# One layer step of a hybrid decoder on one core: x loaded on SyncE's queue, a shorter root in two norms, another order of x1's blocks, unread products, dt's sums in three steps

## The chip, the core and the metric

The kernel runs on one core of a Trainium2 chip. The core has a matmul engine (TensorE, PE in the profile, with its weight loads shown apart as PEld), and VectorE (DVE), ScalarE (ACT) and GpSimd (POOL) for the work on elements; SyncE (SP) only issues transfers. Each engine takes its own instructions in order, and semaphores order the engines against each other. DMA queues belong to the engine that issues into them (SP's, ACT's and POOL's are used here). SBUF and PSUM are the memories on the core: a matmul writes PSUM, which has eight banks in this kernel, four in a pool for the large products (`mm`) and four for the rest (`ms`).

The metric is the device time of one execution in microseconds (us), shorter is better.

## The reference

One step of one layer for 256 prompt tokens and 8 × 8 sample tokens, 320 in all, with a width of 2048, float32 throughout:

```python
h = rms_norm(x, norm_mix_pre)
u, v, z, xbc, dt = split(h @ w_in)            # 2048, 2048, 2048, 3072, 32 columns
gate, chunk_v = chunk_spatial_gate(u, v, ...)  # gelu, layer norm of v, products inside chunks of 128
ssm, states = ssd_mixer(z, xbc, dt, ...)       # conv of 4, softplus of dt, chunked scan, gated norm
x = x + rms_norm(concat(gate, ssm) @ w_out, norm_mix_post)
f = conv_ffn(rms_norm(x, norm_ffn_pre))        # up to 2 x 5632, conv of 3, gelu(g) * u, down to 2048
x = x + rms_norm(f, norm_ffn_post)

def rms_norm(x, w): return x * rsqrt(mean(x * x) + 1e-6) * w
```

Outputs are x, the states of the scan, the last rows of the convolutions and of v.

## The kernel before

Activations lie transposed: 128 of the 2048 features on the partitions, 16 such blocks (kt 0 to 15), the 320 tokens along a row. A product with float32 weights is made from two halves of each operand in the reduced type fp32r: x = hi + lo, w = hi + lo, and `accumulate` (L126) issues three matmuls per block, w_hi·x_hi (L128), w_hi·x_lo (L129) and w_lo·x_hi (L130), each 128 × 128 by 128 × 320. Weights come in slabs by `slab` (L110): SP loads `wraw` (512 KB, or 256 KB for the first four), ACT casts it to `whi` (L117), DVE subtracts to get `wlo` (L119). Each of the three has three buffers, so SP's issue of a slab waits until the slab three before it is split, and the cast waits until PE has used the slab three before.

`project` (L152) multiplies all 16 blocks of the split activations (`h_hi`, `h_lo`) into 4 banks, 2 blocks and 24 matmuls per slab; with `more` it fills 6 banks, and a third slab for every two then serves the two others. `ready` is called ahead of each slab and makes the blocks of activations that the slab needs. `chunk_out` (L199) multiplies 4 blocks of a mixer or FFN result into the 16 blocks of `acc`. Work of the other engines and small products run as background generators, which `tick` moves one step (one `yield`) after a slab. A list scheduler orders each engine's instructions by priority (`first()` and `high_priority` raise it), and `issue_after` adds an order that the data doesn't ask for.

The places that matter here, in order of time:

- **The start.** PE runs `EARLY` matmuls on ones. ACT's queue gets x in six pieces (L526: 1, 1, 2, 4, 4 and 4 blocks, the tile `vt`), SP's the slabs. `x_ready` (L533) scales and splits a block into `h_hi` (ACT, L537) and `h_lo` (DVE, L538) for V0, the first projection (192 matmuls). The norm's factor r1 isn't in these: it's applied when the banks are read out, so V0 can start at once. r1 comes from x by tokens, which POOL loads by `load_by_token` (L548), four pieces of 512 KB and two of 256 KB (`bT`, `cT`), behind `h_hi` of block 8; `with_r1` squares and sums them and spreads r1.
- **dt.** `steps` (L414) makes the step sizes and then three groups of small products: prefix sums `cs_ps` (L463), the same transposed `csT_ps` (L478), and the sums after each token `dec_ps` (L491). A `yield` stands between some of these.
- **Norm 2.** The last `chunk_out` of the mixer calls `squares_of` per block: ACT squares, POOL adds; the last three blocks go a faster way, and block 15's square (L297) stands alone in `one`. `token_sums` (L258) sums both tiles over the features with three small matmuls each (`tsum`), `rsqrt_by_root` (L237) makes 1/sqrt by ACT's Sqrt and one correcting step on DVE, `spread` (L267) turns it into a row by three transposes. `root_table` (L252) activates a Sqrt on one element. A product of the scan's final state (`fin_ps`, L877) and its sum (L879) lie between.
- **x1.** `x1_ready` (L975) makes block kt of x1 = x + norm 2: DVE multiplies (L980), then adds the block of x (`xr`, loaded by SP; DVE for blocks 0 and 1, POOL for the others, L981), then `split` (ACT L346, DVE L347). The first `project` of the FFN takes these as they come, 288 matmuls in 6 banks, with one slab of `ahead`, so blocks 0 and 1 and then 2 and 3 are made together.
- **Norm 3.** The squares of x1 go half to `sq3` (added on POOL) and half to `sq3b` (DVE). `ffn_up(0)` (L1002) multiplies one further bank (`ps_one`, 48 matmuls), takes the sums and the root, reads the banks out with the factor r3, and multiplies the last one (`ps_other`).
- **`renewals`** (L1085), the renewal of the sample states, runs in the background of the FFN. Its tile `kept` has the tag of the mixer's `ohi`, and so its memory; ACT scales parts of it (L1118), and the raw loads come from `xq_d`.
- **The tail.** Norm 4 goes like norm 2, with products `x1p` that bring x1 into PSUM; DVE and POOL finish the blocks and SP and ACT store them.

## Time and profile before

| | |
|---|---|
| runs of the kernel | 1811.83 us median of 3 (1809.76 to 1812.11) |
| the profiled execution | 1812.42 us |
| its span in the trace | 1810.7 us |
| mean granted clock of TensorE | 0.993 |
| matmuls (L128 to L130 alone) | 0.31 us each, pipelined |
| DMA | 306.46 MB, 169 GB/s on the mean |

The span is what the profiler saw from the first to the last instruction; the profiled execution took 1.7 us more than that. Two things in the views need care. Matmuls overlap, so the duration of one (0.31 us) is about twice the distance from one to the next. And "granted clock" is the share of TensorE's full clock that the chip's throttle allowed: 0.50 means that every matmul took about twice as long, with no idle time shown. In a row of the stretches, the columns are the stretch, its length, the busy time and the instructions of PE, PEld, DVE, ACT and POOL, the granted clock, the DMA engines' busy share and GB/s. In a timeline row they are start, duration, engine, line, operation, tiles and shapes, count, and the idle time before it with what ended it. In a row of the costliest groups, the mean duration in ns stands behind the busy time.

### The profile page before, as it was taken

The numbers are of one execution on the slowest core, as the hardware profiler recorded it, in microseconds if no ns is written. First come the engines' busy times: TensorE is split into PE (matmuls) and PEld (weight loads), VectorE is DVE, ScalarE is ACT, GpSimd is POOL, SyncE is SP. The second block draws the span as 40 slices with busy tenths as digits, with TensorE's granted clock in tenths as the row PEclk, the third lists the DMA queues.
The fourth block names the chain that finished last, engine by engine and source line by source line (L and its number), as shares of the span: only waits on it lengthen the run. The fifth ranks groups of instructions, "written<-read, shape, count | busy, mean of one in ns | idle before, by whom it ended". The sixth has DMA issues, their size and how long they took to land.

```text
span 1810.7 us, 31220 instructions
## 1 busy us (share of the span) xinstructions
PE 1784.3 (99%) x12222; PEld 1750.2 (97%) x12222; DVE 1183.4 (65%) x2033; ACT 798.7 (44%) x1106; POOL 303.2 (17%) x624
## 2 busy tenths in 40 slices
PE   8999999999999999999999999999999999999998
PEld 7999999999999898998899999999999999999997
DVE  4449565556867778577776575757665565756575
ACT  6444454334535354445455444344434343433335
POOL 2102110000120111005622212121201020101004
PEclk9999999999999999999999999999999999999999
DMA  8545544445764644454556656565654444444442
GB/s 269 178 149 176 173 137 152 152 151 162 244 197 154 192 161 150 137 178 150 161 163 201 196 191 211 174 202 177 194 175 151 147 153 150 155 152 153 149 153 99
DMA packets 229779, 306.46 MB, mean 169 GB/s; under 512 B 17440, under 2 KB 152704, under 8 KB 229440
## 3 DMA queue, kind: packets, MB, share of 16 engines
q1 hardware_dynamic: 216384, 279.26, 48.5%
q10 hardware_dynamic: 11024, 18.10, 2.7%
q0 software_dynamic: 2224, 7.11, 1.4%
q8 instruction: 96, 1.57, 0.4%
q14 instruction: 51, 0.42, 0.1%
HBM read 286.85 MB, written 17.58 MB: 168 GB/s over the span
## 4 chain that ended last, share of the span: by engine, by line
PE 93%; DVE 2%; DMA 2%; ACT 1%; POOL 1%; issue 1%; ACTq 0%; DVEq 0%; POOLq 0%
PE ps L128 19%; PE ps L130 19%; PE ps L129 19%; PE pd L128 10%; PE pd L130 10%; PE pd L129 10%; DMA wraw<-in_w_in 1%; PE y_ps L851 1%; DVE wlo L119 1%; POOL acc_mix L981 1%; PE yo_ps L804 1%; ACT whi L117 0%; PE sg L658 0%; PE up_ps L1128 0%; PE xt_ps L357 0%
## 5 line engine op out<-in xcount | busy, mean ns | idle before, releaser
L119 DVE TENSOR_TENSOR wlo<-wraw,whi 128x1024 fp32r<-128x1024 f32 (+1 forms) x476 | 591.4, 1243 | 409.1 <-ACT whi L117 406.1
L117 ACT CAST whi<-wraw 128x1024 fp32r<-128x1024 f32 (+1 forms) x476 | 496.8, 1044 | 721.1 <-PE ps L129 443.4
L128 PE MATMUL ps<-h_hi,whi 128*128 128x320 f32 x2528 | 790.2, 313 | 11.0 <-ACT whi L117 7.6
L130 PE MATMUL ps<-h_hi,wlo 128*128 128x320 f32 x2528 | 786.5, 311 | 4.0 <-DVE wlo L119 4.0
L129 PE MATMUL ps<-h_lo,whi 128*128 128x320 f32 x2528 | 785.1, 311 | 0.0
L128 PEld LDWEIGHTS ps<-h_hi,whi 128*128 128x128 f32 x2528 | 477.8, 189 | 17.6 <-ACT whi L117 9.2
L130 PEld LDWEIGHTS ps<-h_hi,wlo 128*128 128x128 f32 x2528 | 477.8, 189 | 6.1 <-DVE wlo L119 5.9
L129 PEld LDWEIGHTS ps<-h_lo,whi 128*128 128x128 f32 x2528 | 477.8, 189 | 1.2 <-issue 0.5
L128 PE MATMUL pd<-fhi,whi 128*128 128x320 f32 x704 | 218.0, 310 | 0.0
L129 PE MATMUL pd<-flo,whi 128*128 128x320 f32 x704 | 217.9, 310 | 0.0
L130 PE MATMUL pd<-fhi,wlo 128*128 128x320 f32 x704 | 217.9, 309 | 0.0
L128 PE MATMUL pd<-ohi,whi 128*128 128x320 f32 x448 | 140.6, 314 | 0.0
L129 PE MATMUL pd<-olo,whi 128*128 128x320 f32 x448 | 139.0, 310 | 0.0
L130 PE MATMUL pd<-ohi,wlo 128*128 128x320 f32 x448 | 138.7, 310 | 0.0
L129 PEld LDWEIGHTS pd<-flo,whi 128*128 128x128 f32 x704 | 132.2, 188 | 0.7
L130 PEld LDWEIGHTS pd<-fhi,wlo 128*128 128x128 f32 x704 | 132.2, 188 | 0.0
L128 PEld LDWEIGHTS pd<-fhi,whi 128*128 128x128 f32 x704 | 132.2, 188 | 0.0
L211 DVE TENSOR_TENSOR acc_ffn<-acc_ffn,pd 128x320 f32<-128x320 f32 x160 | 77.1, 483 | 35.8 <-PE pd L130 34.8
L1032 POOL COPY ptf<-pad 128x2 f32<-128x2 f32 x88 | 23.0, 263 | 390.7 <-DVE pad L1020 390.0
L128 PEld LDWEIGHTS pd<-ohi,whi 128*128 128x128 f32 x448 | 84.1, 188 | 4.0 <-issue 2.5
L130 PEld LDWEIGHTS pd<-ohi,wlo 128*128 128x128 f32 x448 | 84.1, 188 | 0.6 <-issue 0.6
L129 PEld LDWEIGHTS pd<-olo,whi 128*128 128x128 f32 x448 | 84.2, 188 | 0.2 <-issue 0.2
(296 smaller groups left out, 1596.1 us busy)
## 6 DMA issues: line engine op xcount, KB each, us to landing
wraw<-in_ffn_w_up SPq DMA_DIRECT2D x176, 512.0 KB, 3.5
wraw<-in_w_in SPq DMA_DIRECT2D x144, 512.0 KB, 3.5
wraw<-in_ffn_w_down SPq DMA_DIRECT2D x88, 512.0 KB, 3.3
wraw<-in_w_out SPq DMA_DIRECT2D x64, 512.0 KB, 3.3
st<-in_state_ssm SPq DMA_DIRECT2D x64, 256.0 KB, 3.7
out_ssm_state_sample<-st ACTq DMA_DIRECT2D x32, 256.0 KB, 2.5
cs<-dacs_d SPq DMA_DIRECT2D x16, 320.0 KB, 3.5
xr<-in_xT SPq DMA_DIRECT2D x4, 640.0 KB, 4.6
```

The lines of the kernel that those rows point to most:

```text
L117: act.copy(hi[:, :m], raw[:, :m])
L119: dve.tensor_tensor(out=lo[:, :m], in0=raw[:, :m], in1=hi[:, :m].bitcast(F32), op=ALU.subtract)
L128: pe.matmul(ps, whi, xhi, start=first, stop=False)
L129: pe.matmul(ps, whi, xlo, start=False, stop=False)
L130: return pe.matmul(ps, wlo, xhi, start=False, stop=last).ins
L211: dve.tensor_tensor(out=acc[:, nb, :], in0=acc[:, nb, :], in1=ps[:, :NT], op=ALU.add)
L804: pe.matmul(ps_yo[row:row + 32, :256], cms[:, 4 * h + i, :], st[h][:, 256 * r:256 * r + 256], start=i == 0, stop=i == 3, tile_position=(0, ...
L851: pe.matmul(ps[64 * i:64 * i + 64, cols], w(hl), x(hl, m, cpx), tile_position=(0, 64 * i), **flags)
L981: added.append((dve if kt < 2 else pool).tensor_tensor(out=a, in0=a, in1=xr[q][:, k, :], op=ALU.add).ins)
L1032: pool.tensor_copy(ptf[:, k, :], pad[:, 256:258])
```

## The change

It has seven parts.

1. `EARLY` is 8, and a tile `eps` holds the constant for Sqrt.
2. x is loaded inside `x_ready`, on SP's queue, each piece just ahead of the slab that needs it. The loads by token go to SP's queue too: one behind the x of block 8's slab, one behind that of 10, two behind that of 12, the last two after V0's. ACT and POOL issue none. `with_r1` gets a further `yield`.
3. `rsqrt_by_root` takes one sum, which `token_sums` accumulates in two calls (`more`). Sqrt reads it from PSUM with scale and bias, beside a multiply-add and a reciprocal on DVE, and three DVE operations follow. `root_table` is called behind the square of block 12, for both norms, and block 15's square is on DVE.
4. `unread(n)` issues n matmuls on an old mixer tile (`res[2]`), whose result nobody reads: 2 between the sums of norm 2, 11 behind its spread.
5. x1: block 0 is added before block 1 is multiplied (`issue_after(added[0])`), and all adds are on DVE.
6. The squares of x1 are one sum, added on DVE, behind the splits of blocks 11 and 15. In `ffn_up(0)` one bank is copied out by ACT, and spread and read-out stand inside the loop of `ps_other`.
7. dt: three more `yield`s, two ahead of the first sums and one behind them.

As scheduled, SP's order in the start is x0, w0, x1, w1, x2, w2, x3, w3, x4-5, w, x6-7, w, x8-9, w, token 0, x10-11, w, token 1, x12-15, w, tokens 2 and 3, w, `bT`. The prefix sums of dt stay at their place among PE's matmuls, the transposed sums come some 18 matmuls later, the others later still. `kept`'s two first loads stand on SP behind the FFN's fifth slab and ahead of x's third piece (blocks 8 to 11), and wait for PE; ACT has its scaling of `kept` between the splits of x1's blocks 1 and 2.

The diff, with the context cut:

```diff
@@ -26,7 +26,7 @@
...
 EPS = 1e-6
-EARLY = 10
+EARLY = 8
@@ -62,8 +62,10 @@
...
     ones = cp.tile([P, P], F32, name="ones")
+    eps = cp.tile([P, 1], F32, name="eps")
...
         dve.memset(ones, 1.0)
+        dve.memset(eps, EPS)
@@ -232,54 +234,50 @@
...
-    rsqrt_ins, sums_ins = [], []
-    def rsqrt_by_root(rest, ps, scale, rows=P):
-        v = tp.tile([P, 3], F32, tag="rs_v3", name="rs_v")[:rows]
-        r = tp.tile([P, 3], F32, tag="rs_r3", name="rs_r", bufs=3)[:rows]
-        t = tp.tile([P, 3], F32, tag="rs_t3", name="rs_t")[:rows]
-        s = tp.tile([P, 3], F32, tag="rs_s3", name="rs_s")[:rows]
-        dve.tensor_scalar(out=v, in0=rest, scalar1=scale, scalar2=EPS, op0=ALU.mult, op1=ALU.add)
-        dve.scalar_tensor_tensor(out=v, in0=ps, scalar=scale, in1=v, op0=ALU.mult, op1=ALU.add)
-        act.activation(s, v, AF.Sqrt)
-        dve.reciprocal(r, s)
-        dve.scalar_tensor_tensor(out=t, in0=v, scalar=-0.5, in1=r, op0=ALU.mult, op1=ALU.mult)
-        dve.tensor_tensor(out=t, in0=t, in1=r, op=ALU.mult)
-        rsqrt_ins.append(dve.scalar_tensor_tensor(out=r, in0=t, scalar=1.5, in1=r, op0=ALU.add, op1=ALU.mult).ins)
+    rsqrt_ins, sums_ins, spread_ins = [], [], []
+    def rsqrt_by_root(ps, scale):
+        v, r, s = (tp.tile([P, 3], F32, tag=f"rq_{n}", name=f"rs_{n}", bufs=1) for n in "vrs")
+        act.activation(s, ps, AF.Sqrt, scale=scale, bias=eps)
+        dve.tensor_scalar(out=v, in0=ps, scalar1=scale, scalar2=EPS, op0=ALU.mult, op1=ALU.add)
+        dve.reciprocal(v, v)
+        dve.tensor_tensor(out=r, in0=s, in1=v, op=ALU.mult)
+        dve.scalar_tensor_tensor(out=v, in0=s, scalar=-0.5, in1=r, op0=ALU.mult, op1=ALU.mult)
+        rsqrt_ins.append(dve.scalar_tensor_tensor(out=r, in0=v, scalar=1.5, in1=r, op0=ALU.add, op1=ALU.mult).ins)
...
-        there = tp.tile([P, 1], F32, name="root_there", bufs=1)
+        there = tp.tile([P, 1], F32, tag="there", name="root_there", bufs=1)
...
-    def token_sums(*sqs):
-        ps = misc("tsum")
+    def token_sums(sq, ps=None, more=False):
+        begins = ps is None
+        ps = misc("tsum") if begins else ps
         for c, o in enumerate((0, P, NT - P)):
-            for i, sq in enumerate(sqs):
-                ins = pe.matmul(ps[:, c:c + 1], sq[:, o:o + P], ones[:, 0:1], start=i == 0, stop=i == len(sqs) - 1).ins
+            ins = pe.matmul(ps[:, c:c + 1], sq[:, o:o + P], ones[:, 0:1], start=begins and c == 0, stop=not more and c == 2).ins
         sums_ins.append(ins)
-        return ps[:, 0:3]
+        return ps if more else ps[:, 0:3]
...
         for c, o in ((2, NT - P), (0, 0), (1, P)):
-            pe.transpose(ps[:, o:o + P], r[:, c:c + 1].to_broadcast([P, P]), ident)
+            spread_ins.append(pe.transpose(ps[:, o:o + P], r[:, c:c + 1].to_broadcast([P, P]), ident).ins)
...
         if begins:
-            act.activation(total, x, AF.Square)
-        else:
-            sq = tp.tile([P, NT], F32, tag=place[0], name="sq", bufs=place[1])
-            act.activation(sq, x, AF.Square)
-            adder.tensor_tensor(out=total, in0=total, in1=sq, op=ALU.add)
+            return act.activation(total, x, AF.Square).ins
+        sq = tp.tile([P, NT], F32, tag=place[0], name="sq", bufs=place[1])
+        made = act.activation(sq, x, AF.Square).ins
+        adder.tensor_tensor(out=total, in0=total, in1=sq, op=ALU.add)
+        return made
@@ -287,14 +285,19 @@
...
             if nb < KD - 3:
-                add_square(total, acc[:, nb, :], nb == 0)
+                made = add_square(total, acc[:, nb, :], nb == 0)
+                if nb == KD - 4:
+                    root_table(made)
...
                     one.append(tp.tile([P, NT], F32, tag="sq", name="sq", bufs=2))
-                act.activation((one or held)[-1], acc[:, nb, :], AF.Square)
+                if nb < KD - 1:
+                    act.activation(held[-1], acc[:, nb, :], AF.Square)
+                else:
+                    dve.tensor_tensor(out=one[-1], in0=acc[:, nb, :], in1=acc[:, nb, :], op=ALU.mult)
@@ -327,7 +330,7 @@
...
             sp.dma_start(a_bc, ssm_a_log[0:1, :].broadcast_to([P, NH]))
-        there = tp.tile([P, 1], F32, name="r1_there")
+        there = tp.tile([P, 1], F32, tag="there", name="r1_there", bufs=1)
@@ -343,8 +346,9 @@
...
         else:
-            act.activation(hi, x, AF.Copy, scale=scale)
+            made = act.activation(hi, x, AF.Copy, scale=scale).ins
             dve.scalar_tensor_tensor(out=lo, in0=x, scalar=scale, in1=hi.bitcast(F32), op0=ALU.mult, op1=ALU.subtract)
+            return made
@@ -456,6 +460,8 @@
...
             yield
+            yield
+            yield
@@ -472,6 +478,7 @@
...
                 act.activation(ed[s_at], p4[s_at, :, r], AF.Exp)
+            yield
@@ -519,19 +526,17 @@
...
             held = gp.tile([P, 1], F32, name="held")
-            k = 0
             with tc.high_priority(offset=300000):
-                for n in (1, 1, 2, 4, 4, 4):
-                    cs = slice(KD + NT * k if k else 0, KD + NT * (k + n))
-                    act.dma_start(flat[:, cs], xT[:, cs])
-                    k += n
-                    if k == 2:
-                        act.activation(held, ones[:, 0:1], AF.Square)
+                act.activation(held, ones[:, 0:1], AF.Square)
...
                 with tc.high_priority(offset=100000):
+                    cs = slice(KD + NT * k0 if k0 else 0, KD + NT * (k0 + nk))
+                    sp.dma_start(flat[:, cs], xT[:, cs])
+                    for _ in range({8: 1, 10: 1, 12: 2}.get(k0, 0)):
+                        load_by_token()
@@ -545,11 +550,12 @@
...
             by_tok += [(t.rearrange("p k n -> p (k n)")[64:, :D // 2], slice(64, P), slice(NP, NT), 2, i) for i, t in enumerate((bT, cT))]
+            to_load = list(by_tok)
             def load_by_token():
-                for t, _, rows, c, i in by_tok:
-                    pool.tensor_copy(t[:, 0:1], hT[0][:, 8, 0:1][t.shape[0] % P:].bitcast(F32))
-                    pool.dma_start(t, x_tok[rows, D // 2 * i:D // 2 * (i + 1)])
+                if to_load:
+                    t, _, rows, _, i = to_load.pop(0)
+                    sp.dma_start(t, x_tok[rows, D // 2 * i:D // 2 * (i + 1)])
@@ -573,9 +579,12 @@
...
             project(w_in, V0, lambda j, ps: scaled(ps, AF.Gelu, vfs[0][:, j, :]), ready=x_ready, small=4, ahead=0, late=late)
-            load_by_token()
+            with tc.high_priority(offset=100000):
+                while to_load:
+                    load_by_token()
...
             def with_r1():
+                yield
@@ -942,7 +951,6 @@
...
-            root_table(pd_last[-1])
@@ -950,23 +958,33 @@
...
+            def unread(n, behind):
+                ps = misc("unread")
+                with tc.issue_after(behind):
+                    for i in range(n):
+                        made = pe.matmul(ps[:, :NT], res[2][0][:, i % 4, :P], res[2][0][:, i % 4, :], start=True, stop=True).ins
+                return made
...
                 with tc.issue_after(pd_last[-1]):
-                    most = token_sums(sq2)
-                with tc.issue_after(sums_ins[-1]):
-                    ps = token_sums(*one)
+                    sums = token_sums(sq2, more=True)
+                made = unread(2, sums_ins[-1])
+                with tc.issue_after(made):
+                    sums = token_sums(one[0], sums)
...
                     made = next(rest[0])
-                r = rsqrt_by_root(most, ps, 1.0 / D)
+                r = rsqrt_by_root(sums, 1.0 / D)
...
                     r2b = spread(r)
+                unread(11, spread_ins[-1])
...
-            xr, added = {}, []
+            xr, added, whole = {}, [], []
@@ -976,20 +994,19 @@
...
                     a = acc[:, kt, :]
-                    with first() if kt < 2 else tc.high_priority(offset=100000):
+                    with first() if kt < 2 else tc.high_priority(offset=100000), tc.issue_after(added[0] if kt else behind):
                         dve.scalar_tensor_tensor(out=a, in0=a, scalar=col(prm_at["norm"][0] + kt), in1=r2b, op0=ALU.mult, op1=ALU.mult)
-                        added.append((dve if kt < 2 else pool).tensor_tensor(out=a, in0=a, in1=xr[q][:, k, :], op=ALU.add).ins)
-                        split(hT[0][:, kt, :], hT[1][:, kt, :], a, col(prm_at["norm"][1] + kt))
+                        added.append(dve.tensor_tensor(out=a, in0=a, in1=xr[q][:, k, :], op=ALU.add).ins)
+                        whole.append(split(hT[0][:, kt, :], hT[1][:, kt, :], a, col(prm_at["norm"][1] + kt)))
...
             project(ffn_w_up, 0, None, late=up0, ready=x1_ready, after=behind, ahead=1, more=DFF, held=added)
-            sq3b = tp.tile([P, NT], F32, tag="pv", name="sq3b", bufs=4)
-            with tc.issue_after(added[11]):
-                for kt in range(KD):
-                    add_square((sq3, sq3b)[kt % 2], acc[:, kt, :], kt < 2, (pool, dve)[kt % 2], ("pv", 4))
+            for kt in range(KD):
+                with tc.issue_after(added[11]), tc.issue_after(whole[11 if kt < 5 else KD - 1]):
+                    add_square(sq3, acc[:, kt, :], kt < 1, dve, ("pv", 4))
@@ -1049,20 +1066,23 @@
...
                         accumulate(ps[:, :NT], wb(k, 0), hT[0][:, kt, :], hT[1][:, kt, :], kt == 0, kt == KD - 1)
-                    if i == 0:
-                        with first():
-                            r = rsqrt_by_root(token_sums(sq3), token_sums(sq3b), 1.0 / D)
+                up0.append((None, 6, ps))
+                raw = fp.tile([P, NT], F32, name="raw")
+                act.copy(raw, up0[0][2][:, :NT])
+                up0[0] = (None, 0, raw)
                 with first():
-                    spread(r, r3)
-                up0.append((None, 6, ps))
-                for _, j, ps in up0:
-                    evac(j // 4, j % 4, ps)
+                    r = rsqrt_by_root(token_sums(sq3), 1.0 / D)
...
                         accumulate(ps[:, :NT], wb(k, 0), hT[0][:, kt, :], hT[1][:, kt, :], kt == 0, kt == KD - 1)
+                    if i == 0:
+                        with first():
+                            spread(r, r3)
+                        for _, j, up in up0:
+                            evac(j // 4, j % 4, up)
@@ -1145,7 +1165,6 @@
...
                 finish(grow)
-                root_table(pd_last[-1])
@@ -1160,12 +1179,12 @@
...
         with tc.issue_after(pd_last[-1]):
-            most = token_sums(sq4)
+            sums = token_sums(sq4, more=True)
...
         with tc.issue_after(made):
-            ps = token_sums(*one)
-        r = rsqrt_by_root(most, ps, 1.0 / D)
+            sums = token_sums(one[0], sums)
+        r = rsqrt_by_root(sums, 1.0 / D)
...
         with tc.issue_after(made):
```

## The prediction, made before the changed kernel ran

> **What bounds the kernel now.** I read the page first, then who TensorE (PE) waited for, then busy time in stretches, then the timeline of the stretches that are not full. All times are us.
>
> ```profile
> span 1810.7 us, 31220 instructions
> ...
> PE 1784.3 (99%) x12222; PEld 1750.2 (97%) x12222; DVE 1183.4 (65%) x2033; ACT 798.7 (44%) x1106; POOL 303.2 (17%) x624
> ...
> PE 93%; DVE 2%; DMA 2%; ACT 1%; POOL 1%; issue 1%; ACTq 0%; DVEq 0%; POOLq 0%
> ```
> PE is busy 1784.3 of 1810.7, and the chain of work that ended last is 93% PE. So the kernel is bound by its matmuls, and an edit pays only where PE stands idle (26.4 in all) or runs at half clock. The waits of PE say who held it:
> ```profile
> PE ps L128 <- ACT whi L117: 7.6, 4, 3.8
> PE ps L130 <- DVE wlo L119: 4.0, 7, 0.8
> ```
> (total, times, longest). Weight halves that were late cost 11.6 of the 26.4. Stretches of the span say where, and show the granted clock (the column before the last two):
> ```profile
> 5.70:43.40 37.70, 30.50 (x184) 28.54 (x185) 20.53 (x39) 25.20 (x41) 7.89 (x16) 0.95 0.88 276
> 12.24:15.65 3.41, 2.08 (x12) 1.77 (x12) 1.62 (x3) 2.35 (x4) 1.26 (x7) 1.00 0.79 278
> 247.80:251.20 3.40, 3.25 (x26) 2.80 (x27) 2.31 (x7) 1.34 (x3) 0.00 (x0) 0.99 0.50 159
> 250.00:256.00 6.00, 6.00 (x32) 5.92 (x32) 0.70 (x5) 1.28 (x4) 0.47 (x2) 0.72 0.38 118
> 838.29:841.70 3.41, 2.24 (x11) 1.17 (x11) 2.03 (x8) 1.36 (x2) 0.35 (x1) 1.00 0.05 17
> 843.10:896.60 53.50, 48.94 (x289) 47.49 (x290) 42.34 (x51) 26.04 (x44) 34.17 (x35) 0.89 0.52 163
> 905.00:1790.00 885.00, 885.00 (x6017) 883.62 (x6016) 566.81 (x919) 373.86 (x484) 151.90 (x374) 1.00 0.52 168
> ```
> The last row is the ordinary state: no idle time, one matmul per 885/6017 = 0.147. Measured against it, three stretches lose time. The first projection, V0 (5.70 to 43.40), is idle 37.70 − 30.50 = 7.2 and, at a mean clock of 0.95, gives away 1.9 more. The sums of dt (250 to 256) lose (1 − 0.72) × 6 = 1.7 to the clock. The x1 stage (843.10 to 896.60, the first 288 matmuls of the up projection) is idle 4.6 and loses 0.11 × 53.5 = 5.9 to the clock. The rows 247.80 and 838.29 end where the clock drops; they and row 12.24 are cut by the grid of 3.41 on which it changes. (A matmul at half clock takes a little less than twice as long, so below I take nine tenths of the clock terms.)
>
> **The change part by part, the start.**
> ```profile
> 1.13 4.52 PE L70 MATMUL early<-ones 128*128 128x128 f32 x20 [1.13 <-DVE ones L66]
> ...
> 4.21 0.33 ACTq L526 DMA_DIRECT2D vt<-in_xT  x1
> ...
> 4.59 0.56 ACT L537 ACTIVATE h_hi<-vt 128x320 fp32r<-128x320 f32 x1 [1.35 <-DMA vt<-in_xT]
> ...
> 5.71 0.41 PE L128 MATMUL ps<-h_hi,whi 128*128 128x320 f32 x1
> ```
> ACT issues the loads of x before; the issue at 4.21 (0.33) stands in front of its first h_hi at 4.59. With the issues on SP that is gone, and eight warm matmuls end at 1.13 + 8 × 0.452 = 4.75 instead of 5.65. First product at about 4.8: 0.9 earlier (bounds 0.3 and 0.9).
>
> The holes after it are late weights:
> ```profile
> 7.47 7.27 DMA wraw<-in_w_in
> ...
> 17.17 13.20 DMA wraw<-in_w_in
> ```
> The loads of one stretch (9 to 13), those of the start (0 to 34), and the page's groups of the two halves:
> ```profile
> DMA packets 585, 1.60 MB, mean 400 GB/s; under 512 B 55, under 2 KB 55, under 8 KB 585
> ...
> wraw<-in_w_in SPq DMA_DIRECT2D x7, 512.0 KB, 7.3
> acc_mix<-in_x_tok POOLq DMA_DIRECT2D x4, 512.0 KB, 6.9
> ...
> L119 DVE TENSOR_TENSOR wlo<-wraw,whi 128x1024 fp32r<-128x1024 f32 (+1 forms) x476 | 591.4, 1243 | 409.1 <-ACT whi L117 406.1
> L117 ACT CAST whi<-wraw 128x1024 fp32r<-128x1024 f32 (+1 forms) x476 | 496.8, 1044 | 721.1 <-PE ps L129 443.4
> ```
> The chain waits 13.20 for one slab while POOL's loads of x by token run beside it; 9 to 13 moved 400 GB/s (first row), so the engines were full. In the new order of SP's queue each x piece stands just ahead of the slab that needs it, and the four large token loads are spread behind blocks 8, 10 and 12. Up to the last V0 slab that is 4.19 MB of weights, 2.63 of x and 2.10 of tokens, 8.92 MB, or 22.3 at 400 GB/s. Transfers begin near 2.8, so the last slab lands at 25 to 27; cast and subtraction (1.05 and 1.24) make it ready by 29.3, and PE, from 4.8 with 168 matmuls, wants it at 29.5. One hole I do expect: SP holds the fourth slab until the first is split, near 6.3, and transfers then start again some 2 later, so the slab for blocks 4 and 5 is split about 1.3 after PE wants it. Of 7.2 + 0.9 × 1.9 = 8.9, I take 7.6 regained (bounds 8.9, and below nothing, rival 3). Token loads feed the first norm's factor, which no PE wait names; they land earlier than PE's use moves. **Start: 8.5.**
>
> **dt.** The small matmuls of the three sums stood together in the row 247.80 to 251.20, and the drop followed. The order now keeps the prefix sums where they were and puts some 18 wide matmuls before the transposed sums and more before the decay sums. The wait for their input stays. Two more table swaps on ACT lie beside full PE work. I take 0.9 × 1.7 = **1.5** (bounds 0, if the drop stays, and 1.7).
>
> **The hole of norm 2.**
> ```profile
> 836.88 0.49 DVE L211 TENSOR_TENSOR acc_mix<-acc_mix,pd 128x320 f32<-128x320 f32 x1
> ...
> 837.68 0.46 ACT L297 ACTIVATE sq<-acc_mix 128x320 f32<-128x320 f32 x1
> ...
> 838.16 1.28 ACT L245 ACT_TABLE_LOAD   x1
> 838.20 0.83 PE L263 MATMUL tsum<-ones,sq 128*128 128x1 f32 x6 [0.34 <-ACT sq L297]
> ...
> 839.06 0.16 DVE L244 SCALAR_TENSOR_TENSOR rs_v<-tsum,rs_v 128x3 f32<-128x3 f32 x1 [1.01 <-PE tsum L263]
> ...
> 840.51 0.54 PE L271 MATMUL spread<-ident,rs_r 128*128 128x128 f32 x3 [0.52 <-DVE rs_r L249]
> ...
> 841.09 1.00 DVE L980 SCALAR_TENSOR_TENSOR acc_mix<-acc_mix,prm,spread 128x320 f32<-128x320 f32 x2
> 842.01 0.88 DVE L981 TENSOR_TENSOR acc_mix<-acc_mix,xr 128x320 f32<-128x320 f32 x2
> ...
> 843.14 0.64 PE L128 MATMUL ps<-h_hi,whi 128*128 128x320 f32 x1 [2.09 <-ACT h_hi L346]
> ```
> The last square waited on ACT behind a weight cast; on DVE it starts as its block is added, at 837.37, 0.3 earlier. The table load, now behind an earlier square, no longer ends at 839.44, and the Sqrt reads PSUM beside DVE's v and reciprocal, leaving two DVE steps of 0.2 behind it: 0.4 less. Block 0's sum no longer stands behind block 1's product (841.09 holds both): 0.5 less. Two unread matmuls between the sums cost 0.3. So the first product comes **0.9** earlier (bounds −0.2, if the PSUM reads are slow, and 1.4).
>
> [...]
>
> Eleven unread matmuls behind the spread fill 11 × 0.147 = 1.6 of the 2.09, so PE is not thin before the x1 stage. Row 12.24 (12 wide matmuls in one 3.4 step, no drop) and row 838.29 (11, mostly narrow, a drop) bracket it: with the unread ones some 14 wide ones are added to the two 512-wide ones of row 838.29's stretch. I take no drop.
>
> A side effect lies in SP's order: two `kept` loads, issued early before, share a buffer with the unread operand and now wait for the last of them, and ACT's scaling of `kept` stands before h_hi of blocks 2 and 3. They are released near 842, and
> ```profile
> kept<-tote_d SPq DMA_DIRECT2D x1, 128.0 KB, 2.5
> ```
> lands at 844.5; block 2 is split near 846 (three ACT and DVE steps of about 0.5), and PE, 24 matmuls in, wants it at 845.7: 0.5 lost. Behind them on SP stand the x load of blocks 8 to 11 and the slabs; three slabs are loaded by then, 72 matmuls or 10.6 of cover.
>
> **The x1 stage.**
> ```profile
> L119 DVE TENSOR_TENSOR wlo<-wraw,whi 128x1024 fp32r<-128x1024 f32 x12 | 18.2, 1527 | 3.1 <-ACT whi L117 3.0
> L981 POOL TENSOR_TENSOR acc_mix<-acc_mix,xr 128x320 f32<-128x320 f32 x14 | 16.3, 1181 | 10.0 <-DVE acc_mix L980 10.0
> L347 DVE SCALAR_TENSOR_TENSOR h_lo<-acc_mix,prm,h_hi 128x320 fp32r<-128x320 f32 x16 | 13.0, 828 | 1.6 <-ACT h_hi L346 1.6
> ```
> These groups are of 843 to 897. An add is 1.18 on POOL and 0.44 on DVE (842.01); with POOL out, DVE's own work should return from 1.53 to 1.24 (wlo) and from 0.83 to 0.54 (h_lo). DVE then needs 16 × (0.54 + 0.44 + 0.54) + 12 × 1.24 = 39.2 for PE's 288 × 0.147 = 42.4. The squares, which stood among ACT's casts, come behind blocks 11 and 15. So PE sets the pace, with little room: I leave 0.5 for `kept` and 1.3 for late splits and put the stage at 44.2. Of 4.6 + 0.9 × 5.9 = 9.9 that regains 8.1; counted as 53.5 − 44.2 it is 9.3. I take **8.5** (bounds 0 and 9.9). The sum of the squares is one row of 15 adds on DVE, 15 × 0.49 = 7.4, of which eleven follow block 15; they end under ps_one's 48 matmuls or, if later, under ps_other's, and the raw copy of one bank gives these their bank.
>
> **The tail.**
> ```profile
> 1794.13 0.83 PE L263 MATMUL tsum<-ones,sq 128*128 128x1 f32 x6
> ...
> 1794.68 1.28 ACT L245 ACT_TABLE_LOAD   x1
> ...
> 1795.98 0.20 ACT L245 ACTIVATE rs_s<-rs_v 128x3 f32<-128x3 f32 x1
> ```
> The second sum was done at 1794.96; the Sqrt waited for the load. DVE's square, and a Sqrt right behind the sum, bring everything after it forward: **1.2** (bounds 0.8 and 1.7).
>
> Sum: 8.5 + 1.5 + 0.9 + 8.5 + 1.2 = 20.6. The profiled execution took 1812.42 (1.7 outside its span of 1810.7), so 1791.8; against the median, 0.6 lower, 1791.2. I predict 1792.
>
> **The rivals.**
> 1. The clock still falls in the hole of norm 2. For: what separates row 12.24 from row 838.29 is one count of matmuls and their width, and 14 added ones may be too few or lie in the wrong step. Two grid steps at half, less the idle 1.4 in them, lose 0.9 × 0.5 × 5.4 = 2.4, and the unread ones hold PE 1.3 longer: 3.7, so **1795.7**. Chance 0.20.
> 2. DVE becomes the bound of x1. If its work does not speed up without POOL, 16 × (0.54 + 0.44 + 0.83) + 12 × 1.53 = 47.3, with 1.3 around it 48.6 instead of 44.2: **1796.4**. Against: wlo is 1.24 where POOL is quiet. Chance 0.12.
> 3. One queue does not carry what three did. In 450 to 470 SP's queue moved this:
> ```profile
> q1 hardware_dynamic: 3940, 4.93, 76.0%
> ```
> that is 247 GB/s, partly with smaller pieces. At that rate 8.92 MB take 36.1; the last slab is ready near 41 and V0 ends near 45 instead of 35: the start's 8.5 go, and 1 more: **1801.5**. Against: single slabs come at 400 in bursts. Chance 0.10.
> 4. Eight warm matmuls are too few. They last 3.6, and the clock grid of the drops above has steps of 3.41. If the first whole step ends unfilled, the next runs at half and loses 0.9 × 1.7 = 1.5: **1793.5**. Chance 0.08. [...]
> 5. The change does not do what it says: another function takes the Sqrt table out before it is used, and both loads stay: **1794.4**. Chance 0.05.
> 6. Slower. SP must wait, before each slab, for the split of the slab three back. If x pieces and tokens in front stretch a slab's landing, three slabs take one turn of landing + 1.05 + 1.24. At 13.20, the worst above, that is 5.2 a slab against PE's 3.53, and V0 ends near 45, as in 3. Slower needs V0 to end after 58, a landing of about 19; then **1816** or more. Against: 19 is beyond every row, and the queue's order gives no transfer a rival. Chance 0.03.
>
> **How the numbers follow.** My forecast has 0.42, the rivals 0.58. All upper bounds together (9.8, 1.7, 1.4, 9.9, 1.7) give 1787.9; to hold rivals 1 to 5 the range goes to 1802. I take 1787 to 1802; beyond it lie rival 6 and the worse half of 3. This kernel's measurement tells 0.2% (3.6) from no change; only rival 6 and a heap of mishaps come there: faster 0.94, same 0.03, slower 0.03.
>
> **What would show it.** Right: first product before 5.0, no hole over 1.5 in V0, which ends near 35; clock 1.00 behind dt; 11 unread matmuls before a first x1 product 5.4 behind the start of block 15's sum (6.3 before), clock 1.00; wlo near 1.24 in the x1 stage, 44 long; no table load between the sums and either Sqrt. Wrong: 0.50 clock at any of the three places, a slab landing over 13, or h_hi of block 2 waiting more than 1 for `kept`.

## The result, and the profile after

The changed kernel takes 1796.66 us at the median (1795.57 to 1798.03, 4 runs), the kernel before 1811.66 (4 runs by now): a ratio of 0.992, 95% interval 0.9902 to 0.9937, so 15.0 us less. Run again later beside the combined versions below it took 1799.38 against 1810.08, 0.9943 (0.993 to 0.9955). The profiled execution, 1795.57 with a span of 1793.8, is the fastest of its four; it is 16.9 shorter than the profiled one of before. The forecast was 1792, that is 20.6 less.

The changed kernel's page (span, busy time, chain), and who PE waited for (total, times, longest):

```profile
span 1793.8 us, 31222 instructions
...
PE 1777.6 (99%) x12225; PEld 1744.1 (97%) x12225; DVE 1185.7 (66%) x2054; ACT 798.4 (45%) x1106; POOL 276.1 (15%) x591
...
PE 88%; issue 6%; DVE 3%; DMA 2%; ACT 1%; POOL 0%; SPq 0%; DVEq 0%; ACTq 0%; POOLq 0%
```
```profile
PE x1p L1178 <- DVE acc_ffn L1204: 2.4, 2, 2.1
PE ps L130 <- ACT whi L119: 2.0, 2, 1.8
...
PE tsum L261 <- DVE sq L279: 1.0, 1, 1.0
PE ps L132 <- DVE wlo L121: 0.9, 3, 0.4
PE tsum L261 <- DVE sq L302: 0.7, 1, 0.7
```

The late weights fell from 11.6 to 2.9, but two waits of the small sums (`tsum`) for squares are now 1.0 and 0.7, where none was over 0.5 before. The same five places in stretches (PE, PEld, DVE, ACT, POOL; granted clock; DMA share; GB/s):

```profile
836.24:879.80 43.56, 43.16 (x289) 42.38 (x289) 41.09 (x70) 25.59 (x45) 9.78 (x14) 1.00 0.65 199
879.80:889.10 9.30, 8.25 (x58) 7.98 (x58) 7.45 (x20) 5.04 (x9) 3.18 (x10) 1.00 0.45 143
12.24:20.00 7.76, 5.95 (x31) 5.69 (x30) 5.15 (x8) 4.98 (x7) 0.00 (x0) 0.78 1.01 365
...
242.00:256.00 14.00, 13.65 (x93) 12.70 (x94) 7.16 (x17) 9.45 (x14) 1.41 (x4) 1.00 0.45 141
829.77:836.24 6.47, 5.20 (x33) 3.87 (x32) 4.90 (x14) 1.87 (x3) 0.59 (x1) 1.00 0.32 103
```

The x1 stage (first row) went from 53.5 to 43.6 at full clock. dt's stretch (fourth) is at full clock. The start has a hole and a half-clock step of its own (third). The hole of norm 2 (last) is 6.47 from the last mixer matmul to the first x1 product, where it was 6.61.

Where the 16.9 came from, read from the start times of the same instruction in both traces, one execution each:

| up to | before | after | gained so far | this part | forecast |
|---|---|---|---|---|---|
| dt's first sum | 247.95 | 242.35 | 5.6 | 5.6 | 8.5 |
| the scan's first state (`fin_ps`) | 515.2 | 508.6 | 6.6 | 1.0 (dt) | 1.5 |
| last mixer matmul | 836.53 | 829.77 | 6.8 | 0.2 | 0 |
| first x1 product | 843.14 | 836.24 | 6.9 | 0.1 (norm 2's hole) | 0.9 |
| first of ps_one | 896.56 | 879.77 | 16.8 | 9.9 (x1) | 8.5 |
| first of ps_other | 905.3 | 889.1 | 16.2 | −0.6 (norm 3) | 0 |
| end of the span | 1810.7 | 1793.8 | 16.9 | 0.7 (tail) | 1.2 |

### The profile page after: what moved, and what is told of

Its sections match the earlier page's. It is cut to its first block, busy times and chain, and to the rows that moved or that the text cites. A ratio compares the mean times of both kernels' runs of the same rounds, so it can differ in the third digit from the quotient of the medians.

```text
span 1793.8 us, 31222 instructions
## 1 busy us (share of the span) xinstructions
PE 1777.6 (99%) x12225; PEld 1744.1 (97%) x12225; DVE 1185.7 (66%) x2054; ACT 798.4 (45%) x1106; POOL 276.1 (15%) x591
## 4 chain that ended last, share of the span: by engine, by line
PE 88%; issue 6%; DVE 3%; DMA 2%; ACT 1%; POOL 0%; SPq 0%; DVEq 0%; ACTq 0%; POOLq 0%
PE ps L130 18%; PE ps L131 18%; PE ps L132 18%; PE pd L130 10%; PE pd L132 10%; PE pd L131 10%; DVE wlo L121 1%; PE y_ps L860 1%; DMA wraw<-in_w_in 1%; ACT whi L119 1%; PE yo_ps L813 1%; DVE sq L279 0%; DMA wraw<-in_ffn_w_up 0%; PE sg L667 0%; PE up_ps L1148 0%
```

## The experiments

All are edits of the changed kernel. The first eight are one profiled execution each; places in the span are compared, since a single time moves by 2 to 4 us between executions (the changed kernel's runs span 1795.57 to 1798.03 and, on another chip, 1797.73 to 1801.46). The last four were timed together. The twelve ran on three chips, on which the old kernel took 1808.96 (the first four), 1807.94 (the next four) and 1810.08 (the last four).

**The start undone.** `EARLY` is 10; x on ACT's queue in six pieces, tokens on POOL's behind `h_hi` of block 8, one `yield` in `with_r1`: the lines of the diff's part 2 turned back.

> Only the start is undone (10 warm matmuls, x on ACT's queue in six pieces, tokens on POOL's, one yield less). If the start's gain lasts to the end: dt's first sums come 5.6 us later than in the changed kernel (248 instead of 242.3), the span is 1799.4 instead of 1793.8, and the clock falls once near 33. If what is gained at the start is taken back later by work that has to wait anyway (the first norm's factor, dt): below 1796.

dt's first sum came at 245.8, the scan's first state at 512.1 (508.6 in the changed kernel): the start is worth 3.5 here, and it is not taken back. That is less than 5.6 because this execution's old start was itself better: its longest hole was 2.0, not 3.8, and the clock did not fall there. So the 5.6 of the table holds 2.1 that the old start loses in one execution and not in another. The span of 1800.1 agrees with the expectation only by chance, since 2.8 of its 6.3 came later, 1.9 of them in norm 3, where the clock fell.

**No unread matmuls behind the spread.**

```diff
-                unread(11, spread_ins[-1])
```

> The 11 unread matmuls behind norm 2's spread are left out (the 2 between the sums stay); every output is still computed. If they hold the clock: 0.50 for one or two steps of 3.4 us around x1's first products, 1.5 to 3 us longer, a span of 1795.3 to 1797. [...]

The stretch of the first x1 products, first in this kernel, then in the changed one:

```profile
832.00:840.00 8.00, 6.12 (x25) 4.51 (x24) 6.39 (x17) 2.92 (x7) 0.59 (x1) 0.57 0.36 120
```
```profile
832.00:840.00 8.00, 7.44 (x46) 6.09 (x45) 6.42 (x17) 2.25 (x5) 0.59 (x1) 1.00 0.35 119
```

Without them the clock stood at half from 833.0 to 839.8, two steps of 3.4, with a longest gap of PE of 1.9. But it fell before the place of the unread matmuls (the spread is at 834.2): what starts the drop lies ahead of that, from the squares' sums to the root, where both kernels do the same work. In the twelve traces that have the 11, it fell in three (dt together, two small slabs, the changed kernel run again), each time for one step, and stayed full in nine. So the 11 can't save the first step; this trace suggests that they save the second.

That they pay for themselves isn't shown. From the last mixer matmul to ps_one this kernel took 50.6. The changed kernel took 50.0, five others with the 11 and a full clock, which change nothing else there, 50.1 to 50.8, and the three with the drop 51.7 to 52.1, because the 11 then run at half clock ahead of the first x1 product. The span was 1796.6, 2.8 more than the changed kernel's, and so inside the expectation, but only 0.6 of that came here; 2.0 came of norm 3, where the clock fell too. There is one trace without them.

**x1's adds back on POOL.**

```diff
-                        added.append(dve.tensor_tensor(out=a, in0=a, in1=xr[q][:, k, :], op=ALU.add).ins)
+                        added.append((dve if kt < 2 else pool).tensor_tensor(out=a, in0=a, in1=xr[q][:, k, :], op=ALU.add).ins)
```

> Only the adds of x1's blocks 2 to 15 go back to POOL; the later squares, the unread matmuls and the rest stay. If POOL's adds slow DVE and come late: wlo near 1.5 us in the x1 stage, PE idle there 2 to 4 us, perhaps a drop of the clock, the stage 46 to 52 us instead of 43.6. If the squares among the casts were the cause and the adds were not: wlo still slowed, but the stage within 1 us of 43.6.

The groups of the x1 stage (mean ns of one behind the busy time), with POOL's adds, then in the changed kernel:

```profile
L999 POOL TENSOR_TENSOR acc_mix<-acc_mix,xr 128x320 f32<-128x320 f32 x14 | 17.3, 1256 | 9.8 <-DVE acc_mix L998 9.8
L121 DVE TENSOR_TENSOR wlo<-wraw,whi 128x1024 fp32r<-128x1024 f32 x12 | 16.7, 1394 | 1.5 <-ACT whi L119 1.5
L350 DVE SCALAR_TENSOR_TENSOR h_lo<-acc_mix,prm,h_hi 128x320 fp32r<-128x320 f32 x16 | 13.7, 875 | 0.6 <-ACT h_hi L349 0.6
```
```profile
L121 DVE TENSOR_TENSOR wlo<-wraw,whi 128x1024 fp32r<-128x1024 f32 x11 | 13.3, 1217 | 0.0
...
L350 DVE SCALAR_TENSOR_TENSOR h_lo<-acc_mix,prm,h_hi 128x320 fp32r<-128x320 f32 x16 | 8.1, 545 | 1.6 <-ACT h_hi L349 1.6
L999 DVE TENSOR_TENSOR acc_mix<-acc_mix,xr 128x320 f32<-128x320 f32 x15 | 6.6, 483 | 0.0
```

An add of 1256 ns on POOL is one of 483 on DVE, and with POOL's adds gone DVE's own `h_lo` falls from 875 to 545. The stage, from the first x1 product at 835.05 to ps_one at 883.57, was 48.5 instead of 43.6, with the clock full: so the adds carry about 5 of the 9.9. The rest is left to the clock and the squares' place; no run separates these two.

**dt's sums together.** The three `yield`s of part 7 are taken out.

> The three yields in the making of dt are taken out again, so that its three groups of small matmuls stand together. If their standing together makes the clock fall: 0.50 for one step of 3.4 us behind them, 1.0 to 1.5 us longer there, span near 1795. If the drop came of something else (the wait for the sums' input, the state of the clock before): clock 1.00, no more than 0.3 us.

The stretch behind dt's sums of this execution, and of a later one with the same edit (e12, below):

```profile
242.00:248.00 6.00, 6.00 (x46) 5.55 (x46) 2.08 (x8) 1.74 (x5) 0.29 (x2) 1.00 0.36 110
```
```profile
244.00:250.00 6.00, 6.00 (x32) 5.96 (x32) 0.40 (x4) 1.64 (x5) 0.47 (x2) 0.72 0.33 107
```

Together, the clock fell in the second and not in the first. It fell in none of the eleven traces with the sums apart. From the first sum to the scan's first state took 265.7 without a drop and 267.2 with one (as before), against 266.3 apart. So the split costs 0.6 of its own and saves 1.5 where the clock would have fallen, as it did in the old kernel and in one of these two.

**Norm 3's sums later.**

```diff
+                        made = accumulate(ps[:, :NT], wb(k, 0), hT[0][:, kt, :], hT[1][:, kt, :], kt == 0, kt == KD - 1)
+                        if kt == 5:
+                            sixth = made
...
+                    with tc.issue_after(sixth):
+                        sums = token_sums(sq3)
```

> Norm 3's three small sums are put behind the sixth block (18 matmuls, 2.6 us) of ps_one instead of right behind its first matmul. If PE only waited there because the sums stand too early in its order: the wait of 1.0 to 1.5 us for DVE's sum of squares is gone, the clock stays at 1.00 behind it, ps_other begins 7.1 to 7.5 us after ps_one (9.3 in the changed kernel), and the whole is 1.0 to 3 us shorter than runs of the changed kernel in which the clock fell there (1798). If what follows the sums (root, spread, read-out) is what counts: the wait moves to ps_other or the next projection and the time stays.

In the changed kernel the sums stand right behind ps_one's first matmul:

```profile
879.32 1.76 DVE L279 TENSOR_TENSOR sq<-sq,sq 128x320 f32<-128x320 f32 x2
...
879.77 0.31 PE L130 MATMUL ps_one<-h_hi,whi 128*128 128x320 f32 x1
...
881.13 0.83 PE L261 MATMUL tsum<-ones,sq 128*128 128x1 f32 x6 [1.05 <-DVE sq L279]
```

PE holds 1.05 until DVE has added the last square. Behind the sixth block the wait was gone, and ps_other began 8.4 behind ps_one (9.4 in the changed kernel). The 7.1 to 7.5 expected were too few: they count the 48 matmuls alone, and the small sums and the spread take the rest. The clock stayed full; it fell behind this wait in all seven traces beside the changed kernel's first that have it, where ps_other came 11.2 to 14.0 behind ps_one. The span shows none of it (1796.4), because this execution had a hole of 2.6 and a half-clock step at the start.

**Norm 2's order.** One slab's subtraction is put behind block 1's x1 on DVE, and v is computed on DVE before Sqrt, which takes it from SBUF. The lines of the second edit, cut:

```diff
-        act.activation(s, ps, AF.Sqrt, scale=scale, bias=eps)
         dve.tensor_scalar(out=v, in0=ps, scalar1=scale, scalar2=EPS, op0=ALU.mult, op1=ALU.add)
+        act.activation(s, v, AF.Sqrt)
...
```

> Two edits in norm 2: the subtraction of one weight slab comes behind block 1's x1 on DVE instead of between the squares, and DVE's v is computed first and Sqrt takes it from SBUF. If these two explain why the hole gained 0.14 instead of 0.9: the wait for the sum of squares (0.75) falls to about 0.25, r comes 0.7 us earlier, the first x1 product 5.7 to 5.9 us behind the start of the last mixer matmul (6.47 in the changed kernel). The moved subtraction may cost up to 1 us in the x1 stage. If the hole is bound by the steps behind the spread: the first product within 0.2 of 6.47.

The hole in the changed kernel, whose last mixer matmul starts at 829.77:

```profile
829.05 1.23 DVE L121 TENSOR_TENSOR wlo<-wraw,whi 128x1024 fp32r<-128x1024 f32 x1
...
830.20 0.48 DVE L302 TENSOR_TENSOR sq<-sq,sq_ps 128x320 f32<-128x320 f32 x1
...
830.82 0.80 PE L261 MATMUL tsum<-ones,sq 128*128 128x1 f32 x6 [0.75 <-DVE sq L302]
...
832.63 0.26 ACT L242 ACTIVATE rs_s<-tsum,eps 128x3 f32<-128x3 f32 x1 [1.61 <-PE tsum L261]
832.92 0.16 DVE L243 TENSOR_SCALAR rs_v<-tsum 128x3 f32<-128x3 f32 x1 [1.32 <-ACT rs_s L242]
...
836.24 1.15 PE L130 MATMUL ps<-h_hi,whi 128*128 128x320 f32 x6
```

A weight subtraction of 1.23 now stands on DVE ahead of the square's sum, and v waits for Sqrt: the two reads of the sums in PSUM are one behind the other, not side by side. With both undone:

```profile
830.39 0.31 PE L136 MATMUL pd<-h_hi,wlo 128*128 128x320 f32 x1
830.80 0.80 PE L268 MATMUL tsum<-ones,sq 128*128 128x1 f32 x6
...
836.07 1.15 PE L134 MATMUL ps<-h_hi,whi 128*128 128x320 f32 x6
838.39 0.42 PE L135 MATMUL ps<-h_lo,whi 128*128 128x320 f32 x1 [1.18 <-DVE h_lo L357]
```

the sums wait for nothing and the first product comes 5.68 behind the last mixer matmul: the missing 0.8. The moved subtraction then makes h_lo late by 1.18: from the last mixer matmul to ps_one it is 49.9, for 50.0 in the changed kernel, so nothing was won. How the 0.8 divides is seen from two of the combined versions below, which differ by v alone: the hole is 6.46 without it and 6.24 with it. So v first is worth 0.2, and the order on DVE the other 0.6.

**Token loads later.** Only one of the six token loads stays among V0's slabs; the other three large ones follow behind them.

```diff
-                    for _ in range({8: 1, 10: 1, 12: 2}.get(k0, 0)):
+                    for _ in range({12: 1}.get(k0, 0)):
```

> Of the six loads of x by token only one stands among V0's slabs, the other five come behind them, on the same queue. If the token loads are what makes V0's weights late: no hole over 0.5 us in V0 and between 32 and 36, dt's first sums at 240 or earlier (242.3 in the changed kernel). If V0's hole near 13 comes of the fourth slab's wait for a buffer: that hole stays (1 to 2 us), and only the one near 33 goes. The squares of the tokens stand on ACT ahead of weight casts; if they then come late, a new hole near 35 to 45.

No hole over 0.4 was left up to 70, the clock stayed full there, and dt's first sum came at 239.0, with a span of 1792.9 in spite of norm 3's wait (1.9) and its drop. V0's last slab shows why. Its load in the changed kernel (issued at 20.4), and here (issued at 19.5); size, us to landing:

```profile
wraw<-in_w_in SPq DMA_DIRECT2D x1, 512.0 KB, 12.6
```
```profile
wraw<-in_w_in SPq DMA_DIRECT2D x1, 512.0 KB, 6.1
```

It landed at 33.0 there and at 25.6 here. What the DMA engines moved meanwhile, in the changed kernel (two rows) and here (one):

```profile
4.00:14.00 10.00, 8.77 (x53) 7.85 (x51) 5.78 (x12) 5.07 (x10) 2.19 (x9) 1.00 0.90 304
14.00:34.00 20.00, 19.05 (x119) 19.06 (x120) 11.05 (x15) 14.81 (x24) 1.81 (x1) 0.91 1.04 316
```
```profile
14.00:34.00 20.00, 19.75 (x134) 19.40 (x134) 12.14 (x17) 14.67 (x23) 1.80 (x1) 1.00 1.02 335
```

The rate differs little, and SP's loads of the start land in the order of their issue: in the changed kernel all of them, from the first (issued at 0.8, landed at 3.1) to the slab issued at 29.6 and landed at 38.6; here the slabs issued at 7.8, 10.7 and 19.5 landed at 11.8, 17.1 and 25.6. So what counts is what stands ahead of a slab in the queue. The hole near 13 is another matter: it stood in four of the seven executions with the changed start and four small slabs, those in which the slab of blocks 4 and 5 took 5.3 to 5.9 to land (holes of 1.2 to 1.8), and not where it took 3.9 to 4.3, with the same loads ahead of it and an issue between 7.3 and 8.1.

**Two small slabs instead of four** (`small=2`).

> Two instead of four small slabs at the start, so that the first wait for a free buffer holds the slab of blocks 4 and 5 at the split of slab one (about 5.5 us) instead of slab two (7.8). If that wait makes the hole near 13: it goes, against a new one of up to 1 us near 8, and dt's first sums come 0.5 to 2 us earlier than 242.3. If the queue's rate alone makes it (everything is loaded at the same rate whatever the order): the hole stays.

The hole near 13 went and one of 1.1 came at 10.5, another of 1.8 stood at 34 and the clock fell behind it: dt's first sum at 243.0, no earlier than 242.35. Since three of the seven executions with four small slabs lack the hole near 13 too, one trace doesn't show that the buffer's wait made it; it shows only that this order won nothing.

**Combined**, timed beside the changed kernel in five rounds: tokens later and norm 3's sums later; the same with v first; the same with dt's sums together.

> The changed kernel once more, beside the three below on the same chip. Its starts and clock drops differ from one execution to the next; from the looks so far: 1796 to 1798 us, 0.990 to 0.994 of before.

> Token loads behind V0's slabs and norm 3's sums behind the sixth block of ps_one, together. If the start's lateness and the wait for norm 3's squares are what kept the change from its 20 us: no hole over 0.5 us before 60 us, ps_other 8.5 us behind ps_one, clock 1.00 up to the tail, 3 to 5 us below the changed kernel, 1791.5 to 1794. If the two only shift later waits (a drop of the clock elsewhere, the next projection): within 1.5 us of the changed kernel.

> As the one before, and in the three short roots DVE computes v first and Sqrt takes it from SBUF. Sqrt and DVE then need not wait for each other's read of PSUM: 0.1 to 0.3 us less in norm 2's hole and in the tail each, 0.2 to 0.5 us in all; if Sqrt behind v is as late as v behind Sqrt, no difference.

> As e10, with dt's sums together again. In the look with them together the clock stayed at 1.00 there and the stretch from them to the scan's first state was 0.6 us shorter than with them apart. If the clock falls only in some executions: 0.6 us below e10 in those where it doesn't, 1 above in those where it does, so within 1 us of e10 at the median. If standing together makes it fall each time: 0.9 us above e10.

| version (runs) | median (range) | ratio to before (95%) |
|---|---|---|
| changed kernel again (5) | 1799.38 (1797.73 to 1801.46) | 0.9943 (0.993 to 0.9955) |
| tokens and norm 3 later (4) | 1794.78 (1792.98 to 1795.78) | 0.9916 (0.9902 to 0.9929) |
| the same, and v first (5) | 1793.53 (1792.51 to 1796.57) | 0.9914 (0.99 to 0.9927) |
| the second row, and dt's sums together (4) | 1794.2 (1792.51 to 1796.02) | 0.9914 (0.99 to 0.9927) |

The two edits are worth 4.6 on this chip, inside the 3 to 5 expected, and the interval of their ratio lies just below that of the changed kernel. The changed kernel itself was slower than expected here: its profiled execution lost the clock in norm 2's hole for one step and in norm 3 for two. In the profiled execution of the first no hole over 0.7 is left up to 60, and norm 3's stretch is at full clock:

```profile
877.60:886.50 8.90, 8.23 (x59) 8.00 (x58) 8.50 (x21) 4.02 (x6) 2.01 (x10) 1.00 0.46 145
```

Whether v goes first, and whether dt's sums stand together, can't be told at the median. With v first, the stretch from ps_other to the end is no shorter (904.8 for 904.7), so the 0.2 in norm 2's hole is all that it shows. In the profiled execution of the last, a hole came where the late tokens were feared (1.6 up to 40.4), but not as feared, by their squares standing on ACT ahead of a weight cast. The cast started at 39.33, and its slab had landed only at 39.23, 13.6 behind its issue, with late token loads ahead of it on the queue; the first combined version had the same slab at 36.6.

## Why the prediction was right, and where it was not

**The time** is inside the range and above the forecast of 1792, by 4.7 at the median and by 3.6 in the profiled execution. The mechanism held: PE's idle time and half-clock steps were what could be won, and they were won at the places named. The sum came as near as it did partly by luck: five terms brought less than forecast (the start 2.9, dt 0.5, norm 2 0.8, norm 3 0.6, the tail 0.5), and x1's 1.4 more and 0.2 ahead of the last mixer matmul made up for some of it. The profiled execution was also a lucky one in norm 3, as said below.

**The start is the term that was mis-sized**: forecast 8.5, measured 5.6, and 3.5 against the other trace of the old start. Right were the first product (4.75), the one queue as such, and the hole at the slab of blocks 4 and 5 (1.8, forecast 1.3). The step that failed: "so the last slab lands at 25 to 27", from 8.92 MB at 400 GB/s. Measured were 304 GB/s from 4 to 14 and 316 from 14 to 34 with the engines' share at 0.9 to 1.04, and a landing at 33.0: the token loads behind blocks 10 and 12 stand in the queue ahead of weights that PE needs. 400 had been read from a stretch of 4 us (9 to 13 in the old kernel, the engines' share 1.01). And the clock fell for a step behind the start's own hole, which the sum had left out. In the profiled execution PE was late itself by then, so that its wait for the last slab shows as only 0.4; in the changed kernel run again, which had neither the hole near 13 nor this drop, PE waited 1.0 and 0.4 there, and dt's first sum came only 0.8 earlier (241.6). V0's last product started at 38.4, where the prediction had V0's end near 35. With the tokens behind V0 the start gained 9.0 against the old kernel's trace (248.0 to 239.0).

**dt** gained 1.0, forecast 1.5: the drop was avoided, as forecast; the 0.6 that the split costs was not in the sum.

**Norm 2's hole** gained 0.1, forecast 0.9. Each step that was counted is there (block 15's square on DVE, no table load between the sums and Sqrt, block 0 first). What failed is "the Sqrt reads PSUM beside DVE's v and reciprocal": v waits for Sqrt; and the order of the changed kernel on DVE, with a weight subtraction ahead of the square's sum, wasn't priced. Undoing both gave the missing 0.8, of which 0.2 are v's and 0.6 the order's. Counted as the prediction did, from block 15's sum (830.59) to the first x1 product, the hole is 5.65, forecast 5.4, and was 6.26; but the sum itself now starts 0.8 behind the last mixer matmul, where it was 0.35 before.

**x1** gained 9.9, forecast 8.5: the stage is 43.6, forecast 44.2; PE sets the pace with DVE busy 41.1 of it, squares included (forecast 39.2 without them). `kept` came as described: ACT stood 1.6 for it ahead of h_hi of block 2. That is over the 1 that the prediction named as a sign of being wrong, but no idle time of PE over 0.3 followed.

**Norm 3** was costed at nothing: "they end under ps_one's 48 matmuls". The squares do end there, at 881.0, but the small sums stand behind ps_one's first matmul, not behind its last. The cover was never there: a wait of 1.05 in the profiled execution, and 1.4 to 2.6 with the clock's drop in the seven others that have the wait (ps_other 11.2 to 14.0 behind ps_one, where 8.7 was the distance before). So the term is 0.6 lost in the profiled execution, less than norm 2's, but 2.5 or more in those seven, where it is, beside the start, the larger part of the time above the forecast.

**The tail** gained 0.7, forecast 1.2; v waits for Sqrt there too.

**The rivals.** The first (the clock falls in norm 2 all the same) holds in three of the twelve traces, for one step instead of two, at some 1.5 instead of 3.7 up to ps_one. Without the 11 unread matmuls, in the second experiment, the clock fell at 833.0 with a gap of PE of 0.75 ahead of the drop; the longest gap there, 1.9, came behind it. The second did not come. The third (one queue) named the right place: neither 247 nor 400 GB/s, but some 310. The fourth (too few warm matmuls) came in part: the profile shows a full clock only from 5.2 in the profiled execution, 0.4 behind the first product, and 0.9 to 2.2 behind it in seven of the other eleven executions with eight warm matmuls, whose first matmuls took 0.47 instead of 0.31. That costs up to 1.0, an estimate from those 2.2 (0.9 × 0.5 × 2.2; the rival's price was 1.5). It isn't the number of warm matmuls alone, since the start undone, with ten, has it 0.7 behind. The fifth and the sixth did not come: no table load stands between the sums and Sqrt, and no slab of the start took over 13 to land in the profiled execution.

What stays open: why the same loads land 2 us later in some executions, what makes the clock fall at one step of 3.4 and not at another, and whether the 11 unread matmuls are worth their time.

## What to carry to other kernels

Cost a cover by the position of the waiting instruction in its engine's order, not by the length of the work around it: a sum that could hide under 48 matmuls hid under one. Rate a stream of loads by the mean of the whole stretch it has to last (304 and 316 GB/s here, where 4 us had shown 400), and put the loads nobody needs soon behind the ones the bound engine waits for, even on the same queue (V0's last slab then landed 6.1 behind its issue instead of 12.6). Charge matmuls that nobody reads with the time that they take when the clock falls all the same (51.7 to 52.1 here, against 50.6 in the one trace without them). Two engines that read one PSUM tile may be ordered one behind the other in the program that is built (Sqrt's read ended at 832.89, v's began at 832.92 and waited for it); don't count them as parallel without a row that shows it.

## What the runs showed of the hardware

In the first 40 us of the changed kernel and its edits the granted clock fell behind single gaps of PE of 1.8 and 2.6 and stayed full behind others of 1.2 to 2.0, and behind norm 3's wait it stayed full after 1.05 and fell after 1.4 to 2.6. So the same kernel lost it at other places in each execution (the changed kernel: from 15.4 in one profiled execution, near 833 and 884 in the other). A step at half clock lasted 3.4 (15.42 to 18.82 in the changed kernel, granted 0.50), and 128x320 matmuls began every 0.267 in it, 1.8 times the 0.147 of full clock. DVE's `h_lo` on 128x320 elements took 545 ns in the mean of the x1 stage, and 875 with POOL's adds beside it.
